# A third part of the down projection by a second level of seven products, with second-level cells formed on chip

## The chip, the cores and the metric

The kernel runs on one core of a Trainium2 chip. The time is device time in microseconds (us). A core has five engines that work side by side: TensorE (PE, matrix products; PEld is its weight load), VectorE (DVE, elementwise work on one or two tensors), ScalarE (ACT, copies with conversion, activations), GpSimd (POOL, which here mostly issues transfers) and SyncE (SP, which issues most transfers). Matrix products end in PSUM, everything else lives in SBUF, and large intermediates are written to and read from memory by DMA.

## The reference

One residual block over 2048 tokens with 1024 channels, everything in float32:

```
x = x + RMSNorm_post(mixer(RMSNorm_pre(x)))
h = RMSNorm_pre(x)
f = square(relu(h @ w_up)) @ w_down        # w_up 1024 x 4096, w_down 4096 x 1024
x = x + RMSNorm_post(f)
```

The mixer (pooling branch, convolution branch, gates, output projection) is not touched. What matters here is the product with `w_down`: 2048 tokens x 4096 x 1024.

## The kernel before

**Precision.** Each float32 matrix is split into a high part (ScalarE, `nc.scalar.copy`) and a low part (VectorE, a subtraction), and a product takes three passes: high x high, high x low, low x high (`matmuls`, line 268). A "product" of the program (`product`) makes a result of 128 x 1024 (two halves of 512) from 4 contraction chunks of 128: 2 x 4 x 3 = 24 matmuls of 128x512. Before it can run, its weights need one cast and one subtraction of 128x1024, and its two cells of tokens two of each.

**Seven products.** A matrix product is cut into 2x2 blocks and done with seven block products instead of eight (Winograd's form of Strassen's method); they are numbered 1 to 7. Products 1, 2 and 4 need a weight block as it is, 5, 6, 3 and 7 need sums and differences of weight blocks; on the token side sums and differences named t1 to t4 are prepared in the up projection.

**The down projection.** Its contraction of 4096 is cut into 4 slabs (`SLABS`), the tokens into 2 blocks (`NB`, index b), the output into 2 halves (index o). Product i of the first level is a sum over the slabs of one product for each (slab, o, b): 4 x 2 x 2 = 16 products. Products 1 and 2 of the first level are done otherwise: each is a large matrix product, and the seven-product method is applied to it a second time. Such a "part" takes 7 second-level products in two halves each, 14 products in place of 16. Part one is first-level product 1 (`level_product`), part two is first-level product 2 (`level_half`). The order is

part one (14) | products 5, 6, 3 (16 each) | product 7 (14, two were done before the up projection as a filler) | part two (14) | product 4 (16, the last 4 in `at_end`).

**Second-level operands.** Part one's token cells were prepared in the up projection. For part two, `level_cells` loads the cells through POOL's queue in the stages of products 3 and 7, subtracts on VectorE, stores the sums V1 to V4 through POOL's queue, and part two loads them back. The weights' sums for parts one and two come from `level_weights` (half 0 of part two during the first up projection, half 1 during product 3), also kept in memory.

**Background work.** Such work is written as generators in a `Lane`. `bg()`, called after each product, advances each lane by its rate; a generator may ask for a pause of so many calls. `behind()` orders what it emits behind the last marked main-line instruction of the same engine, or of TensorE where that engine has no mark. Instructions inside `tc.high_priority(offset=AHEAD)` are planned as if they stood 260 instructions earlier. A planner puts out a fixed order for each engine, and gives a tile its buffer when the instruction that first writes it comes up; if no buffer of the pool is free there, that instruction waits.

**Buffers.** All tiles are 128x1024 float32. `p_big` (line 769) has 28, `p_tr` 9, `p_fo` 6, `p_wr` (raw weights) 4, `p_wh` and `p_wl` (split weights) 3 each, `p_ws` 2. PSUM has 3 accumulators of 128x1024 and 2 of 128x512. Results of the down projection are held in `p_big`: `c00`, `c01`, `c11` and `u`, each with 4 tiles (2 output halves x 2 token blocks).

**Finishing.** Each token block b has two halves t. `Finish(b, t).steps` takes the four result tiles, squares and sums them, forms the inverse root, multiplies (VectorE, from PSUM), adds x with an accumulating DMA on POOL's queue (line 1951), and stores them with another (line 131). A result's buffer is free when its store has landed. `fin[0, 1]` and `fin[1, 1]` (from `c01` and `c11`) run one behind the other in a lane that starts with part two; `fin[0, 0]` runs in a lane that starts with product 4; the last one, `fin[1, 0]`, is written out by hand in `at_end`. Ahead of it the end loop runs the first output half of the last four jobs, fetches the four x tiles of the last block into `p_big`, and puts the weights of the second output half into `p_big` as well (`weight_down(i, n, 1, BIG)`).

The lines that set where this work goes, before:

```
SHARED, ALONE = (5, 6, 3, 7), (4,)
items = jobs[:at] + HALVES + jobs[at:]
PREPARE = (0, 3, 0)
lanes.append(Lane(1.2, chain_of(level_weights(2, 1, fo), level_cells())))
lanes += [Lane(2, fin[0, 1].steps(2), fin[1, 1].steps(2, 0, 6))]
```

Of the kernel before, what the change touches and what calls it, by code (L numbers as in the profile page):

```python
# [18 lines left out]
T = 512  # L19
# [48 lines left out]
def block_kernel(  # L68
# [1708 lines left out]

    def when_idle(gen, n):
        yield n
        yield from gen  # L1780
# [17 lines left out]
    SHARED, ALONE = (5, 6, 3, 7), (4,)  # L1798
# [8 lines left out]
    def weight_down(i, s, o, home=None):  # L1807
# [14 lines left out]
        with tc.high_priority(offset=AHEAD):  # L1822
# [4 lines left out]
            if i == 3:  # L1827
                return split_w(joined(sub, 1, "sum"))
# [4 lines left out]
    def token_cells(s, i, b, home=TR, hi_home=BIG):  # L1833
# [9 lines left out]
            3: ((1, 1), None),  # L1843
# [41 lines left out]
    def last_product(i, o, b, ps):  # L1885
# [14 lines left out]
        elif i == 6:  # L1900
            u[k], c01[k] = mk(*BIG), mk(*BIG)
            to(u[k], c00[k])
            mark(add(c01[k], u[k], c11[k]))
        elif i == 3:
            to(c01[k], c01[k])
            fin[b, 1].ready[o] = c01[k]
        elif i == 7:
            to(u[k], u[k])
            mark(add(c11[k], c11[k], u[k]))
            fin[b, 1].ready[o + 2] = c11[k]  # L1910
        else:
            to(u[k], u[k])
            fin[b, 0].ready[o + 2] = u[k]

    class Finish:


        def __init__(self, b, t):
            self.b, self.t, self.x, self.ready = b, t, {}, {}
            self.order = (0, 1, 2, 3)  # L1920
# [11 lines left out]
        def steps(self, lag, sooner=0, behind_total=3):  # L1932
            sq = Squares(FO)
# [10 lines left out]
            dg = spread_dve(root_dve(st, q2[self.b, self.t]), FO)  # L1944
# [147 lines left out]
    fin = {(b, t): Finish(b, t) for b in range(NB) for t in (0, 1)}  # L2092
    jobs = [(s, i, b) for i in SHARED for s in range(SLABS) for b in range(NB)]
# [25 lines left out]
    def level_weight(part, p, n):  # L2119

        with tc.high_priority(offset=AHEAD):
            t = mk(p_wr, "wr")
            o = {1: 2 * n, 2: 2 * (n + 2), 4: 2 * (n + 2) + 1}.get(p)
            load(t, level[part, p, n] if o is None else w_down[o, part - 1])
            return split_w(t)

    def level_cell(part, p, u):

        cell, T = {1: ((0, 0), "T"), 2: ((1, 0), "V")}[part]
        b, at, k = {  # L2130
            1: (0, 0, cell), 2: (0, SLABS, cell), 3: (1, SLABS, cell),
            5: (1, 0, T + "1"), 6: (1, SLABS, T + "2"), 7: (1, SLABS, T + "3"),
            4: (1, SLABS, T + "4"),
# [11 lines left out]
    def level_cells():  # L2145

        def get(u, which):
            b, v = {22: (1, u + SLABS), 12: (1, u), 11: (0, u), 21: (0, u + SLABS)}[which]
            t = mk(*(BIG if u % 2 else FO))
            aside(t, fd[b, v, (1, 0)])  # L2150
            return t

        def kept_as(k, v, t):
            fd[1, v, k] = dram("fd")
            aside(fd[1, v, k], t)

        NEED = (22, 12, 11, 21)
        here = {}
        for k in NEED:
            here[k] = get(0, k)  # L2160
            yield
        for u in range(SLABS):
            there = {}
            for k in NEED:
                if u + 1 < SLABS:
                    there[k] = get(u + 1, k)
                if k == 22:
                    t = mk(*(BIG if u % 2 else FO))
                    sub(t, here[22], here[12])
                    kept_as("V3", u + SLABS, t)  # L2170
                elif k == 12:
                    sub(here[12], here[12], here[11])
                    kept_as("V1", u, here[12])
                elif k == 11:
                    sub(here[22], here[22], here[12])
                    kept_as("V2", u + SLABS, here[22])
                else:
                    sub(here[21], here[21], here[22])
                    kept_as("V4", u + SLABS, here[21])
                yield  # L2180
            here = there

# [8 lines left out]
    def level_product(p, w, cells):  # L2191
# [12 lines left out]
        with tc.high_priority(offset=AHEAD):  # L2204
            if p in (1, 5, 6, 4):
                o = taken_of[p] = mk(*BIG)
                mark(nc.scalar.copy(o, ps))
                if p == 4:
                    c00[1, 0] = o
            else:  # L2210
                of, k = {2: (1, (0, 0)), 7: (5, (1, 1)), 3: (6, (0, 1))}[p]
                c00[k] = taken_of[of]
                mark(add(c00[k], ps, c00[k]))
        bg()

    def level_half(p, n, w, cells):
# [8 lines left out]
        if n:  # L2225
            k = {1: (0, 0), 2: (0, 0), 6: (0, 1), 3: (0, 1), 5: (1, 1), 7: (1, 1), 4: (1, 0)}[p]
            with tc.high_priority(offset=AHEAD):
                mark(add(c00[k], c00[k], ps))
# [189 lines left out]
```

## Time and profile before

| | us |
|---|---|
| median of 3 runs | 2155.14 |
| lowest and highest | 2153.99, 2157.71 |
| profiled execution | 2162.05 |
| its span, first to last instruction | 2160.3 |
| TensorE busy in it | 2137.6 |
| VectorE busy in it | 1688.5 |
| ScalarE busy in it | 1045.0 |

The profile comes from one execution. The span is cut into stages by the times at which TensorE goes from one kind of product to the next: part one from 1558 us, product 5 from 1634, product 6 from 1721, product 3 from 1808, product 7 from 1895, part two from 1972, product 4 from about 2048, the hand-written end from 2119. In a group's row stand line, engine, operation, output tile and input tiles, shapes and count, then busy time and mean duration, then the engine's idle time just before, and what ended it. In a timeline a row is a start, a duration, the instruction, and in brackets the idle time before it with what ended that. A line is often that of a helper (268 for every matmul, 118 and 121 for every sum and difference), so that tiles tell more than lines.

### The profile page before, as it was taken

What the parts mean: (1) busy time and instruction counts of PE and PEld (TensorE: products, weight loads), DVE (VectorE), ACT (ScalarE), POOL (GpSimd) and SP (SyncE); (2) the same over time, 40 slices, a digit from 0 to 9 for tenths busy, and PEclk for the clock granted to TensorE, in tenths of its full rate; (3) what the DMA queues carried; (4) which work ended last, traced back from release to release, by engine and by line L of the source; (5) the groups of instructions that cost most, each with busy time, mean ns of one, the idle gap of its engine ahead of it and who ended that gap; (6) DMA issues with size and microseconds to landing.
All of it is one profiled execution on the core that took longest, in us unless ns stands there. A gap on an engine that the chain in (4) does not pass through costs nothing.

```text
span 2160.3 us, 25332 instructions
## 1 busy us (share of the span) xinstructions
PE 2137.6 (99%) x9585; PEld 1769.7 (82%) x9585; DVE 1688.5 (78%) x1655; ACT 1045.0 (48%) x1094; POOL 78.1 (4%) x143
## 2 busy tenths in 40 slices
PE   9999999999999999999999999999999999999998
PEld 7888888888888888888888878888888888888887
DVE  8997789998688998987858784776776657576975
ACT  6444454334543545545644674655663332234761
POOL 1000000000000000000000000000000000120002
PEclk9999999999999999999999999999999999999999
DMA  7688898777997787545787698577697997896877
GB/s 272 243 293 315 326 352 283 253 255 290 340 369 251 253 333 278 193 166 195 289 308 288 238 358 329 212 257 285 258 374 302 348 381 259 336 365 238 299 258 208
DMA packets 173930, 618.40 MB, mean 286 GB/s; under 512 B 19312, under 2 KB 21616, under 8 KB 173808
## 3 DMA queue, kind: packets, MB, share of 16 engines
q1 hardware_dynamic: 143168, 506.44, 64.4%
q0 software_dynamic: 17824, 64.07, 8.4%
q10 hardware_dynamic: 12816, 46.27, 5.5%
q8 instruction: 75, 1.23, 0.2%
q14 instruction: 47, 0.39, 0.1%
HBM read 406.89 MB, written 209.81 MB: 285 GB/s over the span
## 4 chain that ended last, share of the span: by engine, by line
PE 80%; issue 8%; DVE 6%; DMA 5%; ACT 1%; SPq 0%; POOL 0%; DVEq 0%; POOLq 0%; ACTq 0%
PE down L268 20%; PE up L268 19%; PE wo L268 8%; PE ga L268 7%; PE gb L268 7%; PE glu L268 5%; PE B L268 4%; PE rb L268 4%; PE A L268 3%; PE pool L268 3%; DVE big L121 1%; DMA fo<-w_down 1%; DVE y L1002 1%; DMA big<-fd 1%; DMA big<-x1d 1%
## 5 line engine op out<-in xcount | busy, mean ns | idle before, releaser
L268 PE MATMUL up<-big,wh 128*128 128x512 f32 x1792 | 482.7, 391 | 4.7 <-DVE big L121 2.9
L268 PEld LDWEIGHTS up<-big,wh 128*128 128x128 f32 x1792 | 337.2, 188 | 77.0 <-DVE big L121 4.1
L225 ACT CAST wh<-wr 128x1024 fp32r<-128x1024 f32 x196 | 205.9, 1051 | 308.4 <-PE up L268 90.3
L1002 DVE SCALAR_TENSOR_TENSOR y<-v,cst,y 128x1024 f32<-128x1024 f32 x240 | 307.3, 1281 | 2.8
L268 PE MATMUL down<-big,wh 128*128 128x512 f32 x872 | 295.4, 390 | 0.8 <-DVE big L121 0.8
L268 PE MATMUL up<-big,wl 128*128 128x512 f32 x896 | 277.8, 391 | 0.0
L225 ACT CAST wh<-ws 128x1024 fp32r<-128x1024 f32 x128 | 134.5, 1052 | 273.5 <-PE up L268 65.8
L268 PE MATMUL down<-big,wl 128*128 128x512 f32 x688 | 212.1, 389 | 0.0
L268 PEld LDWEIGHTS up<-big,wl 128*128 128x128 f32 x896 | 169.1, 189 | 35.1
L268 PE MATMUL down<-tr,wh 128*128 128x512 f32 x504 | 196.2, 389 | 0.5 <-DVE tr L121 0.5
L268 PEld LDWEIGHTS down<-big,wh 128*128 128x128 f32 x872 | 163.6, 188 | 35.3 <-DVE big L121 1.1
L121 DVE TENSOR_TENSOR wl<-ws,wh 128x1024 fp32r<-128x1024 f32 x120 | 146.5, 1221 | 58.5 <-ACT wh L225 58.1
L121 DVE TENSOR_TENSOR wl<-wr,wh 128x1024 fp32r<-128x1024 f32 (+1 forms) x121 | 146.3, 1210 | 28.2 <-ACT wh L225 27.8
L121 DVE TENSOR_TENSOR big<-big,big 128x1024 fp32r<-128x1024 f32 (+1 forms) x108 | 129.6, 1220 | 37.6 <-ACT big L1137 13.8
L121 DVE TENSOR_TENSOR tr<-tr,big 128x1024 fp32r<-128x1024 f32 x94 | 112.7, 1220 | 54.2 <-ACT big L1864 41.7
L268 PEld LDWEIGHTS down<-big,wl 128*128 128x128 f32 x688 | 129.1, 188 | 26.8
L268 PE MATMUL wo<-big,wh 128*128 128x512 f32 x480 | 128.5, 390 | 0.0
L268 PE MATMUL glu<-big,wh 128*128 128x512 f32 x464 | 125.3, 391 | 1.3 <-ACT big L796 0.8
L1864 ACT CAST big<-tr 128x1024 fp32r<-128x1024 f32 x70 | 72.0, 1048 | 100.0 <-DMA tr<-fd 76.7
L268 PE MATMUL gb<-big,wh 128*128 128x512 f32 x448 | 120.0, 390 | 0.0
L268 PE MATMUL ga<-big,wh 128*128 128x512 f32 x448 | 119.9, 389 | 0.0
L268 PEld LDWEIGHTS down<-tr,wh 128*128 128x128 f32 x504 | 94.6, 188 | 20.6 <-DVE tr L121 1.0
(240 smaller groups left out, 3431.6 us busy)
## 6 DMA issues: line engine op xcount, KB each, us to landing
tr<-fd SPq DMA_DIRECT2D x98, 512.0 KB, 7.8
wl<-kept SPq DMA_DIRECT2D x85, 512.0 KB, 5.0
wr<-w_down SPq DMA_DIRECT2D x80, 512.0 KB, 7.3
kept<-wl SPq DMA_DIRECT2D x72, 512.0 KB, 6.0
wr<-w_up SPq DMA_DIRECT2D x64, 512.0 KB, 4.8
wr<-w_in SPq DMA_DIRECT2D x59, 512.0 KB, 5.5
fd<-tr ACTq DMA_DIRECT2D x54, 512.0 KB, 3.9
big<-fd SPq DMA_DIRECT2D x48, 512.0 KB, 7.1
```

Of the source, the lines that this page charges most:

```text
L121: return nc.vector.tensor_tensor(o, a, b, op=ALU.subtract)
L225: nc.scalar.copy(hi[:, :n], src[:, :n])
L268: i = nc.tensor.matmul(ps, w[wp][:, (at + k) * P : (at + k + 1) * P], rhs[k][xp], start=start and n == 0, stop=stop and n == len(order) - ...
L1002: nc.vector.scalar_tensor_tensor(acc, v[:, k : k + TB], wk, acc, op0=ALU.mult, op1=ALU.add)
L1864: nc.scalar.copy(hi, t)
```

## The change

First-level product 3 becomes part three and is done by a second level of seven products, like products 1 and 2. The order becomes

part one (14) | part two (14) | products 5, 6 (16 each) | product 7 (14) | part three (14) | product 4 (16).

- Part two's and part three's second-level cells are no longer made in the background. `level_formed` loads first-level cells with SP, forms the sums on VectorE when product 6 (and 4) of the part is due, and keeps the ones for products 5 and 7 in buffers (`p_tr`); one of them (V2) is stored and loaded back for product 4. `level_cells` is gone.
- Part three's weights are combinations of stored sums: `level_weights_3` loads, for each half, four weight blocks and four stored sums through POOL's queue, forms eight sums or differences, and stores seven results. It runs in a lane from the first product of the stage of product 7 on, and is emptied before part three.
- `level_weights(2, 1)` moves into the second up projection's background chain.
- Part one's result goes to `u`, part two's to `c00`, part three's is added to `c01`.
- `fin[0, 1]` and `fin[1, 1]` start with product 4, each in a lane of its own, next to `fin[0, 0]`. `fin[0, 1]` takes its temporary tiles from `p_ws`.

```diff
+    def level_weights_3(n):
+        def get(s, o):
+            t, w = fo(), fo()
+            aside(t, w_down[2 * s + o, 1])
+            aside(w, wsum[s, o])
+            sub(t, t, w)
+            return t, w
+        def kept_as(k, t):
+            level[3, k, n] = dram("level")
+            aside(level[3, k, n], t)
+        a21, _ = get(n, 1)
+        yield
+        a22, s5 = get(n + 2, 1)
+        kept_as(4, a22)
+        add(s5, a21, a22)
+        kept_as(5, s5)
+        yield
+        a11, s6 = get(n, 0)
+        kept_as(1, a11)
+        yield
+        sub(s6, s5, a11)
+        kept_as(6, s6)
+        sub(a21, a11, a21)
+        kept_as(7, a21)
+        yield
+        a12, s3 = get(n + 2, 0)
+        kept_as(2, a12)
+        sub(s3, a12, s6)
+        kept_as(3, s3)
+        yield
...
-    SHARED, ALONE = (5, 6, 3, 7), (4,)
+    SHARED, ALONE = (5, 6, 7), (4,)
...
+    fin[0, 1].tmp = p_ws, "ws"
...
+    def level_formed(part, p, n):
+        cell = {2: (1, 0), 3: (1, 1)}[part]
+        units = (2 * n, 2 * n + 1)
+        def get(b, u, home=FO):
+            t = mk(*home)
+            load(t, fd[b, u, cell])
+            return t
+        if p in (5, 7):
+            return [formed.pop((p, u)) for u in units]
+        made = []
+        with tc.high_priority(offset=AHEAD):
+            for u in units:
+                if p in (1, 2, 3):
+                    b, at = {1: (0, 0), 2: (0, SLABS), 3: (1, SLABS)}[p]
+                    x = get(b, u + at)
+                elif p == 4:
+                    x, t = get(0, u + SLABS), mk(*TR)
+                    load(t, fd[1, u + SLABS, "V2"])
+                    sub(x, x, t)
+                else:
+                    t3, t1, x = get(1, u, TR), get(0, u, TR), get(1, u + SLABS)
+                    sub(t1, t3, t1)
+                    sub(t3, x, t3)
+                    sub(x, x, t1)
+                    fd[1, u + SLABS, "V2"] = o = dram("fd")
+                    aside(o, x)
+                    formed[5, u], formed[7, u] = t1, t3
+                made.append(x)
+        return made
...
+    items = halves(2) + first + halves(3) + [job for job in jobs if job[1] in ALONE]
...
-    PREPARE = (0, 3, 0)
+    PREPARE = (0, SHARED[-1], 1)
...
-            if n == at:
-                lanes += [Lane(2, fin[0, 1].steps(2), fin[1, 1].steps(2, 0, 6))]
...
-            lanes.append(Lane(1.2, chain_of(level_weights(2, 1, fo), level_cells())))
+            lanes.append(Lane(1.2, chain_of(level_weights_3(0), level_weights_3(1))))
         if (s, i, b) == (0, ALONE[0], 0):
+            empty()
+            lanes += [Lane(2, fin[0, 1].steps(2)), Lane(2, fin[1, 1].steps(2, 0, 6))]
             lanes.append(Lane(3, fin[0, 0].steps(2, 150)))
...
+            if n + 1 == last:
+                empty()
+                parts_at(last)
+                parts_at(last + 1)
+                weight_at(last)
```

More of the change, by code (lines that the diff above doesn't have):

```diff
@@ L1842, in token_cells @@
             5: ("t1", None) if ready else ((0, 1), (0, 0)),
-            3: ((1, 1), None),
         }[i]
@@ L2301, in block_kernel @@
                 for k in (n + 1, n + 2):
[L2302 to L2303 removed]
+                    weight_at(k)
                 for k in range(n + 1, n + 5):
[L2305 removed]
+                    if is_half(k) or k in (second, last + second) or k < n + 3:
                         loads_at(k)
```

148 lines of the change are left out of this document (59 added, 89 removed).

## The prediction

> **What bounds the kernel now.** I read the page first, then a table of the stages, then the chain that ended last, and only then single engines. The page says that TensorE is busy all the time, and gives 390 ns for a matmul of the down projection.
>
> ```profile
> span 2160.3 us, 25332 instructions
> ...
> PE 2137.6 (99%) x9585; PEld 1769.7 (82%) x9585; DVE 1688.5 (78%) x1655; ACT 1045.0 (48%) x1094; POOL 78.1 (4%) x143
> ...
> L268 PE MATMUL down<-big,wh 128*128 128x512 f32 x872 | 295.4, 390 | 0.8 <-DVE big L121 0.8
> ```
>
> The 390 ns is a latency, not a price: the chain shows what a matmul costs when matmuls follow each other.
>
> ```profile
> 1869.36 5.44 PE rb L268 x24
> 1874.80 16.32 PE down L268 x72
> ```
>
> A product (24 matmuls of 128x512: two output halves, four contraction chunks, three passes) takes 5.44 us, 0.227 us per matmul. With this price the stages of the down projection can be cut out: 14 products are 76.2 us, 16 are 87.0. The rows are most of the second up projection, part one, product 5, product 7, part two, the lone product 4, and the end (busy us and count of PE, weight loads, DVE, ACT, POOL; clock; DMA share; GB/s).
>
> ```profile
> 1240.00:1558.00 318.00, 313.85 (x1390) 259.06 (x1389) 224.77 (x224) 183.85 (x188) 12.79 (x24) 0.99 0.76 282
> 1558.00:1634.20 76.20, 76.20 (x338) 63.10 (x337) 56.87 (x50) 44.42 (x45) 0.00 (x0) 1.00 0.85 332
> 1634.20:1721.30 87.10, 86.34 (x380) 70.98 (x380) 52.19 (x45) 28.66 (x29) 1.59 (x3) 1.00 0.92 349
> ...
> 1895.40:1971.60 76.20, 76.20 (x338) 63.10 (x337) 50.98 (x46) 32.04 (x35) 9.90 (x19) 1.00 0.81 311
> 1971.60:2048.00 76.40, 75.64 (x336) 62.07 (x336) 67.19 (x73) 48.15 (x52) 4.96 (x7) 1.00 0.84 294
> 2048.00:2119.00 71.00, 71.00 (x323) 58.94 (x322) 51.85 (x62) 37.68 (x43) 6.06 (x9) 1.00 0.79 259
> 2119.00:2160.30 41.30, 31.09 (x244) 29.61 (x242) 25.70 (x55) 7.54 (x13) 8.74 (x11) 0.93 0.65 195
> ```
>
> Up to 2119 us TensorE has no hole worth the name, so a product less is 5.44 us less, provided that nothing behind it becomes late. The nearest thing to a limit is VectorE in part two (67.2 of 76.4 us) and, as the last part shows, buffers at the end.
>
> **What is removed.** Product 3 has 4 slabs x 2 token blocks x 2 output halves = 16 products before, and 14 afterwards. All other counts stay. So 2 x 5.44 = **-10.9 us**. The whole gain is this.
>
> **What is moved onto VectorE.** Its price per operation comes from the trace of part two:
>
> ```profile
> 1972.76 0.69 DVE L118 TENSOR_TENSOR big<-big,rb 128x512 f32<-128x512 f32 x1 [2.03 <-PE rb L268]
> 1973.48 1.22 DVE L118 TENSOR_TENSOR big<-big,big 128x1024 f32<-128x1024 f32 x1
> ...
> 1984.78 2.48 DVE L118 TENSOR_TENSOR fo<-fo,fo 128x1024 f32<-128x1024 f32 x2
> 1987.17 1.22 DVE L121 TENSOR_TENSOR tr<-tr,big 128x1024 fp32r<-128x1024 f32 x1
> 1988.31 1.22 DVE L121 TENSOR_TENSOR wl<-wr,wh 128x1024 fp32r<-128x1024 f32 x1
> 1989.44 1.22 DVE L121 TENSOR_TENSOR tr<-tr,big 128x1024 fp32r<-128x1024 f32 x1
> ...
> 1994.59 2.35 DVE L121 TENSOR_TENSOR big<-big,big 128x1024 fp32r<-128x1024 f32 x2
> 1996.86 1.22 DVE L121 TENSOR_TENSOR wl<-wr,wh 128x1024 fp32r<-128x1024 f32 x1
> ```
>
> Starts lie (1996.86 - 1994.59) / 2 = 1.135 us apart. A part now needs, for its 14 products, 28 subtractions that split cells, 14 that split weights, 7 sums from PSUM and 16 that form the second-level cells: 65 x 1.135 = 73.8 us against 76.2 us of TensorE. That fits on average, since the squares and sums of two output blocks (the fo rows, which made the splits of 1987 and 1989 late) leave part two: the 0.76 us hole of that stage (76.40 - 75.64) goes, **-0.8 us**. It doesn't fit at the start, since the order is 1, 2, 6, and product 6 needs 12 of the 16 formations. Before the sixth product of a part (5 x 5.44 = 27.2 us after the start) VectorE must do the splits of products 3 to 6 (8 for cells, 4 for weights), 12 formations and 1 sum: 25 x 1.135 = 28.4 us. For part two some of it can be done ahead, under the last product of part one, whose result ScalarE copies. Between 0 and 4 us (if the loads come late as well) I take **+1.5 us**. For part three the last sums of product 7 come first (0.69 and 1.22, the first two rows), background work is ordered behind them, and another sum and weight split are due: 28.4 + 1.9 + 2.3 = 32.6 against 27.2, so 5.4 us by VectorE alone; 0 if the planner puts the formations late enough.
>
> **What is moved onto the DMA queues.** The stage of product 7 before:
>
> ```profile
> GB/s 142 331 331 387 402 295 387 419 421 419 419 417 421 419 417 419 417 413 424 417 424 415 411 245 338 176 342 413 428 419 421 385 22 0 144 131 0 0 0 0
> DMA packets 6499, 23.69 MB, mean 311 GB/s; under 512 B 727, under 2 KB 727, under 8 KB 6495
> ```
>
> About 420 GB/s is the ceiling here, and half of the stage lies on it. Afterwards the stage carries 30 transfers for its own weights and cells, 30 on POOL's queue for the weights of part three (per half: 8 loads, 7 stores; each reads a weight block and a stored sum), and 10 for the first cells of part three: 70 x 0.524 = 36.7 MB, where 420 GB/s x 76.2 us allow 32.0. The 4.7 MB left over are 11 us of transfers, which fall on the start of part three, where the 12 loads of product 6 wait. So the entry of part three costs between 0 and 11 us; by the nearest row (VectorE, 5.4) less what can be prepared early I take **+4 us**.
> That transfers on POOL's queue hold up SP's can be seen already (the first row is the stage of product 7, the second the time from 2040 us on; the last number is us to landing):
>
> ```profile
> wr<-w_down SPq DMA_DIRECT2D x9, 512.0 KB, 10.8
> ...
> wr<-w_down SPq DMA_DIRECT2D x13, 512.0 KB, 4.2
> ```
>
> The Trainium skill ("DMA: Bandwidth & Descriptors", Issuing engines are not separate DMA queues) has DMAs of all issuing engines run on the same 16 DMA engines and interleave; by that rule, with which the two rows agree, POOL's queue is no side road, and the sum would hold the 11 us in place of the 4, about 2176: rival D.
>
> In the up projection, 4 more loads, 4 stores and 4 sums or differences join; VectorE is busy for 224.77 of 318 us there, and nothing waits for them until part two: 0, at most 1 us if that cover is gone.
>
> **What is moved to the end.** The first-half results of both token blocks were finished (squares, root, multiply, add x, store) during part two and product 4. Now all of it starts with product 4, and there the buffers are the matter. The pool "big" has 28. At 2099 us before, these are held: 4 of the block being finished, 4 of the next, 4 results of the last block, 6 cells of the end loop, 2 of its first weight: 20. Then x takes 4, the last cells 2, the next weight 2: exactly 28.
>
> ```profile
> 2098.94 1.21 DVE L124 TENSOR_TENSOR big<-big,rb 128x1024 f32<-128x1024 f32 x1
> 2099.44 1.86 SPq L127 DMA_DIRECT2D big<-x1d  x4
> 2102.29 1.04 ACT L225 CAST wh<-wr 128x1024 fp32r<-128x1024 f32 x1
> 2105.56 1.98 ACT L1864 CAST big<-tr 128x1024 fp32r<-128x1024 f32 x2
> 2107.45 1.05 ACT L225 CAST big<-wr 128x1024 fp32r<-128x1024 f32 x1
> 2120.80 1.05 ACT L225 CAST big<-wr 128x1024 fp32r<-128x1024 f32 x1 [12.30 <-DMA out<-big]
> ...
> 2125.90 1.22 DVE L121 TENSOR_TENSOR big<-wr,big 128x1024 fp32r<-128x1024 f32 x1
> ```
>
> The third weight waits 12.3 us until a store of the finished block has freed a buffer, and the fourth is split at 2125.9 to 2127.1, just ahead of its use: the end's 96 small matmuls of the first half run from 2119.18 to 2130.70, 24 per weight, so the fourth is needed at 2127.8.
>
> ```profile
> 2119.18 0.28 PE L268 MATMUL down<-big,big 128*128 128x256 f32 x1
> ...
> 2130.70 0.62 PE L723 MATMUL rb<-fo,ones 128*128 128x512 f32 x2
> ```
>
> After the change two blocks, not one, are unfinished there: 4 buffers more, 32 wanted where 28 exist. By its lane (rate 2) the first of them multiplies after the first product of the end loop, one product later than the block did before; the second has a pause of 6 in place of 3 and multiplies only behind the loop's last product. POOL's queue takes them in order:
>
> ```profile
> 2100.82 0.89 POOL L1951 DMA_DIRECT2D big<-x1d  x1 [46.26 <-DVE big L124]
> ...
> 2119.98 0.53 POOL L131 DMA_DIRECT2D out<-big  x1 [1.98 <-DMA big<-x1d]
> 2134.07 0.90 POOL L1951 DMA_DIRECT2D big<-x1d  x1 [13.55 <-DVE big L124]
> ...
> 2148.86 0.53 POOL L131 DMA_DIRECT2D out<-big  x1 [2.08 <-DMA big<-x1d]
> ```
>
> A block takes 14.8 us (second pair of rows) to 19.2 us (first) from its first add to its last store. On the clock of before: first block's last store at 2119.98 + 5.44 = 2125.4; second block's at 2125.4 + 0.6 + 14.8 = 2140.8 at the earliest; its buffer is free 5.9 us later (2119.98 to 2125.90 before), the split takes 1.2: 2147.9 for the fourth weight that is needed at 2127.8. That is **+20 us**, or +24.5 with 19.2. It holds if x takes the four free buffers at 2099, ahead of the last cells; the rows speak for it, as x is issued at 2099.4 and the cells are cast at 2105.6, behind a weight cast that has to wait for the same product as x. If the cells and weights win, only x comes late: its loads would go out as the second block's stores land, at 2141 to 2147, take 8.0 us, and the last half of the end would be held up by some 2 to 8 us; that is the low end, +2.
>
> ```profile
> big<-x1d SPq DMA_DIRECT2D x4, 512.0 KB, 8.0
> ```
>
> Sum: -10.9 - 0.8 + 1.5 + 4 + 20 = **+13.8 us**. The profiled execution took 2162.05 us around its span of 2160.3, so 2175.9 for it. The runs shown have a median of 2155.14, 0.3% below; on that scale 2168.9, **2169 us**.
>
> **Rivals.** *A, the forecast, 50%*: the end waits for buffers, 2160 to 2182. *B, x waits in place of cells and weights, 22%*: -11.7 + 5.5 + 2 = -4.2, 2151, from 2147 to 2155. For it: cells and weights are asked for with priority, x without. Against it: the order of 2099.4 and 2105.6. *C, the two products come out whole, 18%*: the planner places formations behind the splits that are due and the finishing work ahead of the end loop, so only -11.7 to -8 remains, 2143.5 to 2147. For it: averages of 73.8 of 76.2 us on VectorE, and 25 to 35 us of VectorE idle in the stages of products 7 and 5. Against it: the formations stand at the start of a part, and a product 7 stage at the DMA ceiling. Its point of decision: both blocks' stores must land by 2127 on the clock of before. *D, the DMA backlog of 4.7 MB lands on part three in full, on top of A, 10%*: 11 in place of 4, and 24.5 in place of 20: 2180.4, up to 2190 if the end's transfers are held up too. For it: half of the stage at the ceiling already. Against it: POOL's transfers for late products can slip without anyone waiting.
>
> **Numbers.** B's middle lies at the limit of what a measurement of this kernel can tell from no change (0.2%, 4.3 us): half of it is faster. Faster: C 0.18 + half of B 0.11 = 0.29; same: the rest of B, 0.11; slower: A and D, 0.60. The range for 8 in 10 cuts the best part of C and the upper half of D: 2146 to 2183. A's own range is 2160 to 2182.
>
> **What would show it.** Product 3's stage must be 76.2 us of matmuls. The formations: holes in TensorE 15 to 30 us after the start of parts two and three that end with VectorE subtractions of tr or fo tiles; no holes there would prove the 5.5 us wrong. The backlog: about 420 GB/s through the whole stage of product 7. The end: casts into big tiles that wait for stores of out, more than the 12.3 us of before, and a hole in TensorE between the end loop and the last half products. If that hole is missing, the forecast is wrong by its largest term, and the change is faster.

## The result, and the profile after

The changed kernel takes 2219.28 us (median of 4 runs, 2217.13 to 2225.45) against 2154.56 us (4 runs, 2153.57 to 2157.71) for the kernel before on the same chip: a ratio of 1.0295, 95% interval 1.0279 to 1.0311. It is 64.7 us slower, where 14 were forecast.

One row of the page of after (its span is 2217.5 us), and then TensorE's work by stage (a window, its length, then busy us and count of PE, weight loads, DVE, ACT, POOL, the granted clock, the share of the DMA engines, GB/s). The rows are part one, part two, products 5 and 6, product 7, part three, and product 4 with the end; the last cut is set by counting matmuls, to within a few.

```profile
PE 2140.5 (97%) x9537; PEld 1768.2 (80%) x9537; DVE 1738.9 (78%) x1699; ACT 1062.8 (48%) x1112; POOL 81.3 (4%) x149
...
1552.10:1628.50 76.40, 76.40 (x339) 63.24 (x339) 57.79 (x61) 47.42 (x49) 0.00 (x0) 1.00 0.84 328
1628.50:1725.90 97.40, 80.55 (x338) 64.74 (x337) 78.16 (x68) 40.62 (x42) 2.13 (x4) 0.93 0.76 292
1725.90:1900.00 174.10, 174.10 (x770) 144.16 (x769) 106.13 (x90) 55.20 (x56) 5.36 (x10) 1.00 0.86 328
1900.00:1976.20 76.20, 76.20 (x338) 63.10 (x337) 51.88 (x45) 20.96 (x21) 12.92 (x24) 1.00 0.83 303
1976.20:2082.50 106.30, 85.65 (x344) 68.35 (x344) 84.82 (x75) 53.92 (x57) 3.21 (x6) 0.87 0.79 301
2082.50:2217.50 135.00, 103.76 (x552) 89.32 (x550) 86.39 (x138) 52.03 (x66) 19.74 (x26) 0.89 0.67 194
```

Same stages before, from the prediction's rows and its cuts: part one 76.2, a product of 16 87.1, product 7 76.2, part two 76.4, and product 4 with the end 71.0 + 41.3 = 112.3. So the 48 matmuls are gone (9585 to 9537), and whatever TensorE runs without a pause costs the same as before: part one, products 5, 6 and 7. All the loss lies in three places: the two parts with formations (97.4 and 106.3 us for 76.2 us of matmuls) and the end (135.0 against 112.3).

TensorE's timeline of after shows what fills them. The number in brackets is the idle time ahead of the row, and behind the arrow what ended it. These are all its holes in the down projection but five, of 0.78 us or less each (together 2.2 us):

```profile
1646.78 0.98 PE L268 MATMUL down<-big,wl 128*128 128x512 f32 x3 [0.51 <-DVE wl L121]
1653.46 1.65 PE L268 MATMUL down<-big,wh 128*128 128x512 f32 x6 [2.27 <-ACT wh L225]
1658.24 0.96 PE L268 MATMUL down<-big,wl 128*128 128x512 f32 x3 [3.13 <-DVE wl L121]
1710.99 0.80 PE L268 MATMUL down<-big,wh 128*128 128x512 f32 x1 [10.29 <-ACT big L218]
1712.44 2.50 PE L268 MATMUL down<-big,wh 128*128 128x512 f32 x5 [0.65 <-DVE big L121]
1992.63 2.93 PE L268 MATMUL down<-big,wh 128*128 128x512 f32 x6 [11.02 <-ACT wh L225]
2018.03 2.93 PE L268 MATMUL down<-big,wh 128*128 128x512 f32 x6 [5.76 <-ACT wh L225]
2067.12 2.07 PE L268 MATMUL down<-big,wh 128*128 128x512 f32 x4 [3.36 <-DVE big L121]
2152.07 0.80 PE L268 MATMUL down<-big,wh 128*128 128x512 f32 x1 [7.53 <-ACT big L1895]
2174.61 0.58 PE L268 MATMUL down<-big,big 128*128 128x256 f32 x1 [7.32 <-ACT big L225]
2182.63 1.22 PE L268 MATMUL down<-big,big 128*128 128x256 f32 x4 [6.37 <-DVE big L121]
```

The account, made over the down projection alone, from its first matmul to the end of the span, since that stretch can be compared from run to run: before 2160.3 - 1557.9 = 602.4 us, after 2217.5 - 1552.1 = 665.4, so +63.0. The holes add up to 60.4 us after and 3.2 before: +57.2. Two products less: -10.9. That leaves 63.0 - 57.2 + 10.9 = 16.7 us in which TensorE was busy but slow. Most of it is the clock. These are the stretches of after with half the clock under running matmuls (as above, the granted clock is third from the end):

```profile
1704.20:1717.85 13.65, 6.21 (x14) 4.54 (x15) 11.35 (x11) 5.88 (x6) 0.00 (x0) 0.50 0.45 154
1984.10:1997.75 13.65, 5.12 (x12) 4.05 (x13) 12.46 (x13) 3.88 (x4) 0.08 (x1) 0.50 1.01 395
2014.82:2021.65 6.83, 3.62 (x9) 2.65 (x9) 6.80 (x7) 6.28 (x8) 1.06 (x2) 0.50 0.43 173
2066.01:2072.84 6.83, 5.52 (x12) 3.94 (x13) 6.73 (x6) 6.83 (x8) 0.00 (x0) 0.50 0.40 120
2147.93:2158.17 10.24, 5.64 (x12) 4.10 (x13) 4.26 (x4) 3.14 (x3) 0.53 (x1) 0.50 0.50 203
2171.83:2185.48 13.65, 4.50 (x19) 4.21 (x20) 3.74 (x4) 2.09 (x2) 4.85 (x7) 0.50 0.98 243
```

They begin in the holes of 10.3, 11.0, 5.8 and 3.4 us in the parts, and in those of 7.5 and of 7.3 and 6.4 us at the end. Each time the clock stays at 0.50 for some us after work has returned: TensorE works for 30.6 us in the six. The six matmuls of the row at 1992.63 take 2.93 us; less the 0.80 us of a single one (row at 1710.99), that is 0.43 us from one start to the next in place of 0.227. By this price 30.6 x (1 - 0.227 / 0.43) = about 14.4 us are lost, some 2.4 for each of the six. What the remaining 2.3 us are isn't shown.

The profiled execution of before, 2162.05 us, lies 7.5 us above the median of its runs; only this one has a profile, so where it lost them isn't shown. TensorE's first matmul of the down projection comes at 1557.9 us in the profile of before, at 1552.1 in that of after, and at 1551.0 to 1559.3 in the profiles of the experiments, all of which have the work that the change adds ahead of it. So this stretch varies by 8 us from profile to profile, and the comparisons below give the down projection's length beside the time.

**Whose wait each hole is.** The exit of part two first: ScalarE around its end, then one row of VectorE:

```profile
1705.47 1.04 ACT L225 CAST wh<-ws 128x1024 fp32r<-128x1024 f32 x1 [7.63 <-DVE ws L118]
1708.94 1.04 ACT L1895 CAST big<-big 128x1024 fp32r<-128x1024 f32 x1 [2.43 <-DVE big L121]
1709.89 3.88 ACT L218 CAST big<-fo 128x1024 fp32r<-128x1024 f32 x4
...
1692.13 2.36 DVE L121 TENSOR_TENSOR fo<-fo,tr 128x1024 f32<-128x1024 f32 x2
```

The `fo` cells of the part's last products had been formed by 1694.5, but their casts (line 218) come at 1709.9. Ahead of them on ScalarE, in the planned order, stand a weight cast and a token cast of product 5, whose own inputs VectorE delivers 7.6 and 2.4 us late. ScalarE took its casts in that order: 10.3 us of TensorE's time go to two casts that product 5 needed only later.

The entry of part three: SyncE's queue, the largest of its waits for 1940 to 2030 us (total, times, longest), then an operation of the lane on VectorE, and the weight cast on ScalarE that ends the hole:

```profile
1947.32 36.27 SPq L127 DMA_DIRECT2D fo<-fd  x8
1983.64 0.44 SPq L127 DMA_DIRECT2D wr<-level  x1
...
SPq L127 <- DMA level<-fo: 21.2, 5, 9.9
...
1979.75 1.22 DVE L121 TENSOR_TENSOR fo<-fo,fo 128x1024 f32<-128x1024 f32 x1 [6.32 <-DMA fo<-wsum]
...
1991.54 1.04 ACT L225 CAST wh<-wr 128x1024 fp32r<-128x1024 f32 x1 [9.98 <-DVE big L121]
```

Eight loads of cells into `fo` tiles take SyncE 36.27 us to issue, because the six `fo` buffers are also those of the weight lane, which gives one back only when its store into `level` has landed. The second weight load of part three (`wr<-level`; the first had gone out at 1939.3) stands behind them in the same queue. It goes out at 1983.6, 7 us after the part's stage began, and lands 7.8 us later, at 1991.5. A second chain ends at the same moment, and it is the one that the profile names: the lane's operation on VectorE stood 6.32 us for a load of its own into `fo`, behind it stood the read-outs of product 7, and behind those the splits of cells of part three, which end at 1991.5 too. The two ends lie 0.04 us apart, so the trace can't tell which of them held the cast; both go back to the lane and its `fo` tiles. The DMA engines moved 303 GB/s in the whole stage of product 7, below the 420 of before's busiest slices; but behind it, while the queue caught up, they were full (395 GB/s, share 1.01, in the second of the six rows above).

The holes at 1653, 1658 and 2018: VectorE has no pause around them (the first two rows begin and end a run of 17 operations without one, from ahead of the hole at 2018 to behind it). On ScalarE the weight casts (line 225) stand behind work that waits for VectorE: ahead of the hole at 1653 behind cell casts (line 218) that wait for formations, ahead of the hole at 2018 behind the reading of a finished result (line 754) that waits for its sum:

```profile
2000.81 1.22 DVE L118 TENSOR_TENSOR big<-big,down 128x1024 f32<-128x1024 f32 x1 [1.17 <-PE down L268]
...
2019.36 1.22 DVE L121 TENSOR_TENSOR wl<-wr,wh 128x1024 fp32r<-128x1024 f32 x1
```

```profile
1651.41 1.04 ACT L218 CAST big<-fo 128x1024 fp32r<-128x1024 f32 x1 [4.75 <-DVE fo L121]
1652.37 2.94 ACT L225 CAST wh<-wr 128x1024 fp32r<-128x1024 f32 x3
...
2013.67 1.06 ACT L754 ACTIVATE ws<-big 128x1024 f32<-128x1024 f32 x1 [3.56 <-DVE big L118]
```

The end: SyncE, ScalarE, and the adds and stores of the two blocks that are finished there on POOL's queue.

```profile
2129.53 1.86 SPq L127 DMA_DIRECT2D big<-x1d  x4
...
2150.97 1.04 ACT L1895 CAST big<-tr 128x1024 fp32r<-128x1024 f32 x1 [14.31 <-DMA out<-big]
...
2173.51 1.04 ACT L225 CAST big<-wr 128x1024 fp32r<-128x1024 f32 x1 [8.70 <-DMA out<-big]
2182.55 1.04 ACT L225 CAST big<-wr 128x1024 fp32r<-128x1024 f32 x1 [7.99 <-DMA out<-big]
...
2130.93 0.91 POOL L1979 DMA_DIRECT2D big<-x1d  x1 [110.55 <-ACT big L796]
...
2149.96 0.53 POOL L131 DMA_DIRECT2D out<-big  x1 [2.07 <-DMA big<-x1d]
2164.13 0.89 POOL L1979 DMA_DIRECT2D big<-x1d  x1 [13.64 <-DVE big L124]
...
2180.30 0.53 POOL L131 DMA_DIRECT2D out<-big  x1 [2.03 <-DMA big<-x1d]
```

x takes four buffers at 2129.5, and from then on every cast into a `big` tile waits for a store of a finished block: cells, third weight, fourth weight.

### The profile page after: what moved, and what is told of

Same layout as the page of the kernel before. It is cut to its first block, busy times and chain, and to the rows that moved or that the text cites. A ratio compares the mean times of both kernels' runs of the same rounds, so it can differ in the third digit from the quotient of the medians.

```text
span 2217.5 us, 25356 instructions
## 1 busy us (share of the span) xinstructions
PE 2140.5 (97%) x9537; PEld 1768.2 (80%) x9537; DVE 1738.9 (78%) x1699; ACT 1062.8 (48%) x1112; POOL 81.3 (4%) x149
## 4 chain that ended last, share of the span: by engine, by line
PE 82%; DVE 8%; DMA 5%; issue 3%; ACT 1%; POOL 0%; SPq 0%; DVEq 0%; ACTq 0%; POOLq 0%
PE up L268 25%; PE down L268 19%; PE gb L268 7%; PE ga L268 7%; PE wo L268 6%; PE glu L268 5%; PE B L268 4%; PE A L268 3%; PE pool L268 2%; PE rb L268 2%; DVE big L121 1%; DMA fo<-wsum 1%; DVE tr L121 1%; DVE y L1002 1%; DVE wl L121 1%
## 5 line engine op out<-in xcount | busy, mean ns | idle before, releaser
L225 ACT CAST wh<-wr 128x1024 fp32r<-128x1024 f32 x210 | 220.1, 1051 | 326.4 <-PE up L268 77.8
L268 PE MATMUL down<-big,wh 128*128 128x512 f32 x1032 | 331.4, 399 | 41.1 <-ACT wh L225 19.0
L268 PEld LDWEIGHTS down<-big,wh 128*128 128x128 f32 x1032 | 198.5, 193 | 86.0 <-ACT wh L225 20.3
L121 DVE TENSOR_TENSOR wl<-wr,wh 128x1024 fp32r<-128x1024 f32 (+1 forms) x135 | 162.7, 1210 | 32.8 <-ACT wh L225 30.9
L121 DVE TENSOR_TENSOR wl<-ws,wh 128x1024 fp32r<-128x1024 f32 x112 | 136.6, 1220 | 50.2 <-ACT wh L225 50.1
L268 PE MATMUL down<-tr,wh 128*128 128x512 f32 x376 | 147.4, 392 | 0.5 <-DVE tr L121 0.5
L121 DVE TENSOR_TENSOR tr<-tr,big 128x1024 fp32r<-128x1024 f32 x68 | 81.8, 1221 | 45.4 <-ACT big L1895 41.3
L1895 ACT CAST big<-tr 128x1024 fp32r<-128x1024 f32 x58 | 60.0, 1049 | 97.3 <-DMA tr<-fd 61.7
L121 DVE TENSOR_TENSOR big<-big,big 128x1024 fp32r<-128x1024 f32 (+1 forms) x80 | 95.7, 1219 | 13.0 <-ACT big L1137 6.4
L268 PEld LDWEIGHTS wo<-big,wh 128*128 128x128 f32 x480 | 89.9, 188 | 19.7 <-ACT tr L1378 1.1
```

What stands on the lines that cost most here:

```text
L121: return nc.vector.tensor_tensor(o, a, b, op=ALU.subtract)
L225: nc.scalar.copy(hi[:, :n], src[:, :n])
L268: i = nc.tensor.matmul(ps, w[wp][:, (at + k) * P : (at + k + 1) * P], rhs[k][xp], start=start and n == 0, stop=stop and n == len(order) - ...
L1895: nc.scalar.copy(hi, t)
```

## The experiments

Each is the changed kernel with the edit shown, leaves nothing of the result out, and ran once beside the kernel before, unless an interval is given. "Down" is the length of the down projection's stretch as in the account above, after the change 665.4 us.

**x of the last block fetched behind the end loop.**

```diff
-            self.fetch(self.order)
...
     empty()
+    fin[1, 0].fetch(fin[1, 0].order)
     at_end(fin[1, 0], w, end)
```

> Changed kernel, with the four x tiles of the last block fetched behind the end loop instead of in its first step. Buffer theory (x takes the four free big buffers first, so the last cells and weights wait for stores): of the four holes of TensorE at the end (7.5, 0.5, 7.3 and 6.4 us) the one before the last cells goes and those before the third and fourth weight shrink to under 3 us together; x lands late and costs up to 8 us at the last sums; the time falls by 10 to 20 us, to about 2200 to 2209. Rival, POOL's queue is simply too slow for three blocks: the holes stay and the time stays within 5 us of 2219.

2206.7 us, down 651.9. The holes of 7.53, 7.32 and 6.37 us are gone; in their place x itself is late:

```profile
2190.74 1.87 PE L2041 MATMUL rb<-inv_d,fo 128*128 128x1 f32 x8 [10.15 <-ACT fo L2031]
```

So it was x's four buffers that the cells and weights lacked. Half of their 22 us comes back, as the price of fetching x behind the blocks' stores.

**The weight lane of part three begun earlier.**

```diff
-    PREPARE = (0, SHARED[-1], 1)
+    PREPARE = (2, 6, 0)
```

> Changed kernel, with the lane that makes part three's weights started two jobs before the end of product 6 instead of at the start of product 7. Theory of held buffers (the lane's fo tiles are held until their stores land, and SP, which issues in order, stands behind a load of a first-level cell that wants one): the 11.0 us hole after part three's first product and the 5.8 us one after it shrink to what VectorE needs, 0 to 5.4 us together; time down by 12 to 20 us. Rival, VectorE's count of operations at the start of a part: the holes stay at 5 us and more each, as those operations are not moved. Rival, the DMA rate: a part of the stall shows up in product 6 or 7 instead.

2221.63 us, down 663.2. Nothing is gained, where 12 to 20 us were expected. (`(2, 6, 0)` is the fourth job from the end of product 6, where the expectation has the second.) The 11.0 us hole at the entry of part three is gone, but TensorE now stops in the second product of the stage of product 7:

```profile
1919.01 0.77 PE L268 MATMUL rb<-big,wh 128*128 128x512 f32 x1 [7.80 <-DVE big L118]
```

VectorE stood at subtractions of the lane whose loads were late (6.82 us up to 1896.8 and 1.60 us up to 1909.1), was busy without a pause from there on, and the read-out of TensorE's accumulator stood behind that work. The lane doesn't hold up whoever comes at a certain time; it holds up whoever stands behind it.

**Token cells asked for no earlier than two items ahead.**

```diff
-                    if is_half(k) or k in (second, last + second) or k < n + 3:
+                    if is_half(k) or k < n + 3:
                         loads_at(k)
```

> Changed kernel, with the first token cells of products 5 and 4 asked for two products ahead like all others, instead of up to four. Theory of the order on ScalarE (the planner put product 5's and product 4's first casts ahead of the casts of the part's last cells, and ScalarE works in order): the 10.3 us hole at the last products of part two goes, and the 3.4 us one of part three; time down by 12 to 18 us. Rival, those cells come late because the stored sum V2 is loaded back late: the holes stay within 2 us of what they were.

2198.23 us, down 641.7; it gained 21 us, more than the 12 to 18 expected. The exit of part two costs 0.59 + 0.76 us in place of 10.29 + 0.65, and the 3.36 us at the exit of part three are gone. The hole at part three's entry fell too, from 11.02 to 7.28. This one condition cost 23.7 us of the down projection: 18.7 of holes, and nearly all the rest is the slow clock behind them (21.1 us of TensorE's work at half the clock are left of 30.6, which is 4.5 us by the price above). That is more than the two products were worth.

**These three together, finishing lanes started sooner.** The lanes' starts in full, with rate 3 in place of 2:

```diff
-            lanes += [Lane(2, fin[0, 1].steps(2)), Lane(2, fin[1, 1].steps(2, 0, 6))]
+            lanes += [Lane(3, fin[0, 1].steps(1, 150, 2)), Lane(3, fin[1, 1].steps(1, 150, 3))]
```

> Changed kernel with the three edits of the runs before, and with shorter pauses in the two finishing lanes (rate 3 instead of 2, pauses 2 and 3 before the root instead of 3 and 6, 1 instead of 2 behind it), so that their stores come out earlier. If the three kinds of hole are independent and are the whole loss, what stays is the gain of two products and the 6 us of VectorE at the start of part two: 2143 to 2153 against 2154.6 before. If the holes only move (VectorE or the DMA rate are the real bound), it stays above 2165.

2198.85 us, ratio 1.0208 (1.0191 to 1.0225), down 644.2. The end keeps a single hole, of 6.0 us, but the early lane now makes one hole of 22.4 us, again in the second product of the stage of product 7. The time is above the 2165 that spoke for holes that only move. So the early lane is no cure; the next run leaves it out.

**Token cells late, x late, finishing lanes with rate 3.** As the run before without the early lane, and the lanes with `steps(2, 150, 2)` and `steps(2, 150, 3)`.

> Changed kernel, with the late token cells (the run that gained 21 us), x fetched behind the end loop, and finishing lanes of rate 3 with pauses 2 and 3 before the root (2 behind it as in the changed kernel), the weight lane in its place. The two holes of the last run that the moved weight lane and the shortened pause behind the root made (22.4 and 6.0 us) go; the end has less than 4 us of holes; left are about 13 us of holes at part two's and part three's start and the 7 to 11 us after part three's first product: 2172 to 2184. If the end's holes come back at 10 us or more, the buffers are not what sets the end.

2184.32 us, down 628.5, holes 27.8, of which 9.64 + 5.73 at the entry of part three, 4.7 at that of part two, and 5.7 at the end, where under 4 were expected. The 10.15 us that late x cost by itself are gone, with the finishing lanes that start sooner.

**Cells loaded straight into their `big` tile.** Plain cells (products 1 to 3 of the parts) skip `fo` and are split in place.

```diff
-                    x = get(b, u + at)
+                    x = mk(*BIG, F32R)
+                    load(f32(x), fd[b, u + at, cell])
...
-                split_of[n] = [split(x, *BIG) for x in loads[n]]
+                p = items[n][2]
+                split_of[n] = [
+                    parted(mk(*BIG, F32R), x) if p in (1, 2, 3) else split(x, *BIG)
+                    for x in loads[n]
+                ]
```

> Changed kernel, with the plain first-level cells of products 1, 2 and 3 of parts two and three loaded straight into a big buffer and split in place, so that they no longer compete with the weight lane for the 6 fo buffers; the lane stays where it is, with all its transfers and all its VectorE work. Theory of held fo buffers: the 11.0 us hole after part three's first product falls below 4 us, the 5.8 us hole stays (VectorE); time down by 8 to 15 us from 2219. Rival, DMA rate: the hole stays above 8 us, as the bytes are the same. Against the theory too: SP may now stand behind big buffers instead, with a hole of the same size.

2212.48 us, down 658.6. The down projection is 6.8 us shorter, below the 8 to 15 expected. At the entry of part three there are six small holes of 8.7 us together where there were 11.02 + 0.32 + 5.76 = 17.1: the `fo` buffers that the cells and the lane share made about half of that. What is left ends with VectorE or the weight casts, and VectorE still stands at subtractions of the lane (11.16 us up to 1955.4, 4.14 us up to 1973.8). The rate of the DMA engines as such, the rival, would have left a hole of more than 8 us, as the bytes are the same; the largest is 3.38.

**Another order of the seven products, first try** (1, 2, 5, 3, 6, 7, 4 in place of 1, 2, 6, ...): product 5 needs 4 of the 16 formations where product 6 needs 12, so that they are spread.

```diff
-    LEVEL = ORDER
+    LEVEL, SMOOTH = ORDER, (1, 2, 5, 3, 6, 7, 4)
...
+                elif p == 5:
+                    t3, x = get(1, u, TR), get(0, u, TR)
+                    sub(x, t3, x)
+                    formed[1, u], formed[3, u] = x, t3
...
-        return [("half", part, p, n) for p in LEVEL for n in (0, 1)]
+        return [("half", part, p, n) for p in SMOOTH for n in (0, 1)]
```

> Changed kernel, with the products of parts two and three in the order 1, 2, 5, 3, 6, 7, 4, so that of the three formations per unit one comes due with product 5 and two come due four halves later. Theory of VectorE's count (25 operations of 1.135 us in 27.2 us of TensorE): the holes at the third pair of products, 5.9 us in part two (0.5 + 2.3 + 3.1) and 6.1 in part three (0.3 + 5.8), fall to under 2 us each; time down by 10 to 16 us from 2219, as a hole also costs clock. Rival, loads that land late: the holes stay at 4 us and more each.

2219.18 us, down 666.3: nothing gained, where 10 to 16 us were expected. The three holes at the entry of part two are gone, but others stand behind them:

```profile
1667.61 2.90 PE L268 MATMUL down<-big,wh 128*128 128x512 f32 x6 [7.55 <-DVE big L118]
1692.98 1.62 PE L268 MATMUL down<-big,wh 128*128 128x512 f32 x6 [1.41 <-DVE big L118]
```

In this order three pairs of neighbours (5 and 3, 6 and 7, 7 and 4) sum in the same PSUM accumulator, and the second waits until VectorE has read the first (the `big` sums of line 118): 1.41 us where VectorE is free, 7.55 where formations stand ahead of the read. So the run could not tell the two theories apart.

**The order 1, 2, 5, 6, 3, 7, 4**, where only 7 and 4 meet in one accumulator.

> Only the order of the seven products is changed, to 1, 2, 5, 6, 3, 7, 4: product 5 needs only 4 of the 16 formations (b0 - b1 differences) and products 6 and 3 share the rest. The count of matmuls, of VectorE operations and of transfers is that of the changed kernel. My theory, that the holes 18 to 30 us behind the start of parts two and three (2.27 + 3.13 and 0.32 + 5.76 us) come from VectorE having 12 formations ahead of the third product, expects each pair to fall under 2 us, one hole of about 1.4 us at the last pair of products (7 then 4 accumulate in the same banks, as in the order 1, 2, 5, 3, 6, 7, 4 that was run before), and the first holes of the parts (0.5 and 11.0), the exit holes (10.3 and 3.4) and the holes of the end (21.7) to stay: 2206 to 2214 us. Rival: these holes come from loads that land late, whatever is formed from them; then the sum of the holes 15 to 35 us behind the part starts stays at 4 to 12 us, and the time at 2216 to 2222.

2214.87 us, down 653.8. In this run the down projection begins 7.2 us later than in after, so the time misses its expectation by 1 us, while the down projection is 11.6 us shorter. The rows of the two entries:

```profile
1665.09 0.50 PE L268 MATMUL down<-big,wh 128*128 128x512 f32 x1 [0.96 <-DVE big L121]
1671.90 0.50 PE L268 MATMUL down<-big,wh 128*128 128x512 f32 x1 [1.00 <-DVE big L121]
...
2014.70 0.97 PE L268 MATMUL down<-big,wl 128*128 128x512 f32 x3 [1.70 <-DVE wl L121]
...
2027.18 0.50 PE L268 MATMUL down<-big,wh 128*128 128x512 f32 x1 [1.08 <-DVE big L121]
```

2.0 us where there were 5.9, and 3.0 (with a hole of 0.17) where there were 6.1, for the same operations and transfers. The first hole of part three stays (8.86 us), and 7 and 4 make one of 1.41. So it was the concentration of the formations ahead of the third product that made the larger part of these holes, not their number and not the loads.

**All of it:** straight loads, this order, late token cells, late x, finishing lanes `Lane(3, fin[0, 1].steps(2, 0, 2))` and `Lane(3, fin[1, 1].steps(3, 0, 4))`.

> All at once: the plain cells of products 1 to 3 loaded straight into big buffers (as in the run called direct), the order 1, 2, 5, 6, 3, 7, 4, token cells asked for only three products ahead, x of the last block fetched behind the end loop, and the two finishing lanes ordered to start sooner after each other. If the causes found are all there are, the holes left are: part entries under 2 us (part two) and under 4 us (part three), 1.4 us at 7 then 4, under 2 us between the end loop and the last halves, plus up to 5 us where x lands late: 10 us of holes and little loss of clock, against 3.2 in the kernel before, so 2154.5 - 10.9 + 7 to 14 = 2151 to 2162 us. Rival: the work that no longer stalls TensorE at one place stalls it at another, since VectorE's load over a part (73.8 of 76.2 us) and the transfers of the product 7 stage are the same; then the holes sum to 20 to 35 us as in the runs before, and the time is 2165 to 2185.

2176.32 us (4 runs) against 2156.81 (7 runs), ratio 1.0089 (1.007 to 1.0109). The rival was right: 22.6 us of holes are left, none over 2.2 us but one of 7.83 at the finishing of a block, and down is 621.4 us, 19.0 more than before. The same account: -10.9 for the products, +19.4 for holes, which leaves 10.5. TensorE works for 13.3 us at half the clock in three stretches, which is 6.3 of it by the price above; the other 4.2 aren't explained. That one hole, on VectorE:

```profile
2117.01 1.22 DVE L121 TENSOR_TENSOR big<-wr,big 128x1024 fp32r<-128x1024 f32 x1 [8.19 <-DMA out<-big]
...
2119.29 0.68 DVE L691 TENSOR_TENSOR fo<-ident,sq 128x512 fp32r<-128x512 f32 x1
```

It is the buffers of the end again. The split of the second half's weight waits for a cast that waits for a store, and behind it in VectorE's order stands the small operation (line 691) that TensorE needs for the second block.

**The same with x at its old place.**

> As direct_in_order, but x of the last block is fetched at its old place, ahead of the end loop. By the buffer theory the four big buffers that x takes are again short for the cells and weights of the last half products: a hole of 6 to 9 us for a cell or a weight cast that waits for a store of out comes back, unless the earlier finishing lanes have freed buffers by then, and the hole for x (up to 10 us in the run that moved x alone) goes. 5 to 15 us slower than direct_in_order if the buffers decide; within 3 us if the earlier lanes have freed them.

2180.88 us, down 626.0, that is 4.6 more, just under the lower expectation. The cells wait again (6.73 us, ACT, line 1895), and VectorE's hole is gone: the shortage moves between the takers of the 28 buffers.

## Why the prediction was wrong

The direction was right and the size was not: 2169 forecast, 2219 measured, 36 us above the top of the range. By its own terms:

- **"So 2 x 5.44 = -10.9 us"**: right. 48 matmuls are gone, and stages without a hole have the length that the price of 0.227 us gives.
- **The old hole of part two goes, -0.8**: that 0.76 us hole went with the old place of part two, but a part that "fits on average" was not for that free of holes: part two now has 16.9 us of them.
- **The entry of part two, "I take +1.5 us", between 0 and 4**: the mechanism was right, the size not. The three holes are 5.9 us. I counted VectorE alone. The trace has a second engine in the chain: a weight cast on ScalarE stands behind a cell cast that waits for a formation, so the weights are late along with the cells. The run with the order 1, 2, 5, 6, 3, 7, 4 brought it to 2.0 us.
- **The entry of part three, "+4"**, from VectorE's 5.4 and the backlog of 4.7 MB: the figure of 5.4 for VectorE came out close (0.32 + 5.76 = 6.1), though less what could be prepared early it went into the sum at 4 with the backlog. The backlog, however, was not the main cause. I had the stage of product 7 at 420 GB/s throughout and rival D at 11 us; it ran at 303, with the loads issued late. What held part three up by 11.0 us more was the lane: its six `fo` buffers, shared with the part's cells, stopped SyncE's queue with the weight loads behind, and its operations stood in VectorE's order ahead of the read-outs. "POOL's transfers for late products can slip without anyone waiting" was the false sentence: they hold buffers and VectorE as they slip. The straight loads took 8.4 us of the entry away, and so bear out the buffers; how the rest divides was not separated.
- **The exits of both parts**: there is no term for them. The holes of 10.29, 0.65, 3.36 and 0.20 us make 14.5. I looked at what the change orders first, the formations, and not at the condition by which the token cells of the *next* stage are asked for up to four products ahead, and what that puts before what on ScalarE. It is a line of the change.
- **The end, "+20 us", with the block at 14.8 to 19.2**: right in its mechanism and, in part by luck, in its size. 7.53 + 0.46 + 7.32 + 6.37 = 21.7 us of holes, the blocks' 19.0 and 16.2 us from first add to last store (2130.93 to 2149.96, 2164.13 to 2180.30), x ahead of the cells as read from the rows of before, and the casts waiting for `out`. Fetching x late made these holes go, as it must by this step. But the sum had the second block's first add at the earliest 0.6 us behind the first block's last store; it came 14.2 us behind, since VectorE's multiply was late (13.64 in the row at 2164.13), and the hole of 7.53 lies inside the end loop, where the sum had none. Rival B (x waits instead) is what that run then showed: 10.2 us, above the 2 to 8 that I gave it.
- **The up projection, 0**: no run contradicts it; the spread of 8 us from run to run would hide 1 us.
- **The clock**: no term at all. Every hole was priced at its length, and 16.7 us came on top, 14.4 of them by the half clock.

The sum with the measured terms: -10.9 + 5.9 + 6.1 + 11.0 + 14.5 + 22.5 (the end with a last hole of 0.78) + 0.4 (a hole behind the last product) - 3.2 (the holes of before) + 16.7 = 63.0. In the order of size the misses are TensorE's slow time, mostly the clock (16.7), the exits (14.5), part three's entry (11.0 and 6.1 against the 4 taken) and part two's entry (4.4).

Whether the change can pay is not settled. With five repairs it still loses 0.9%. Two things weren't tried: room for four more tiles in `p_big`, and part two at its old place behind product 7 with the new part three elsewhere.

## What to carry to other kernels

When work on a full engine is traded for operations on a half-idle one, put each queue's order at the seams on paper, entry and exit: which instruction of the next stage stands ahead of the last ones of this stage on ScalarE, VectorE and SyncE, and what it waits for. A background lane that shares a buffer pool with the main line is not in the background, since its buffer comes free only when its store has landed, and one load that waits for it holds up the whole queue. Price a hole in TensorE above its length: here some 2.4 us more for each long one.

## What the runs showed of the hardware

The lost clock was not expected. Behind the long holes it was 0.50 for 3.6 to 6.2 us of matmuls (the six rows of the result). Short holes differ: behind those of 2.27 and 3.13 us in part two it stayed at 1.00, while in the run with all repairs it fell behind a single hole of 2.15 us that ended at 2041.3.

The clock records of the twelve traces tell them apart. Within each trace all changes of the clock lie whole multiples of 3.413 us from one another (in after at 1704.20, 1717.86, 1984.10, 1997.75, 2014.82 and so on). I cut the down projections into stretches on this grid, up to the last 9 us of each. Of 57 drops, 53 stand at the end of a stretch in which TensorE was idle for 60% of the time or more, the other four at 35 to 52%; no stretch idle for more than 55% is without a drop. The clock came back only at the end of a stretch with at most 17% idle. By this a hole of 2 to 3 us costs clock when it lies within one stretch, and none when it is cut in two. The first two rows are stretches of after: they hold the end of the hole of 2.27 us and the two pieces of that of 3.13. The last two are of the run with all repairs: the stretch with its hole, and the one behind it:

```profile
1653.00:1656.41 3.41, 1.65 (x6) 1.05 (x6) 3.41 (x4) 2.31 (x3) 0.00 (x0) 1.00 0.34 138
1656.41:1659.83 3.42, 1.59 (x7) 1.33 (x8) 3.42 (x4) 2.74 (x3) 0.54 (x1) 1.00 0.38 139
```

```profile
2038.40:2041.81 3.41, 1.26 (x6) 0.78 (x5) 3.41 (x4) 1.84 (x3) 0.00 (x0) 1.00 0.73 175
2041.81:2045.22 3.41, 3.41 (x9) 2.65 (x8) 1.81 (x3) 3.41 (x5) 0.00 (x0) 0.50 0.81 286
```

The Trainium skill ("TensorE: Matmul & The Clock Gate", Part 1: The HAM clock gate) says that the clock halves after an idle window of about 3.4 us, comes back after about as long a busy one, and that the window runs freely. The halving, the length of 3.41 us and the fixed grid agree with the rows here. Beyond it, the rows show that TensorE need not be idle for the whole of a window: 1.26 us of work in 3.41 did not keep the clock.
